# Eighteen more expert tiles' first products made in the gate stage, their outputs kept in device memory until the expert loop

## The chip, the cores and the metric

The kernel runs on one core of one Trainium2 chip. The metric is the device time of one execution in microseconds (us), as the median of a few runs. The core's engines work side by side, each through its own instructions in order: PE (TensorE, the matmuls), PEld (its weight loads, which overlap the matmuls), DVE (VectorE), ACT (ScalarE), POOL (GpSimd) and SP (SyncE, which here only issues DMA transfers). ACT and POOL issue some transfers too. All transfers run on 16 DMA engines.

## The reference, cut to what matters

Two transformer blocks follow one another on 512 tokens of 1024 features. The change touches the last part of the first block, a layer of 16,384 experts of which each token uses 128:

```python
q = einsum('bsd,dq->bsq', h, w_q).reshape(b, s_len, 8, 2, 128)
scores = einsum('bshpc,hpnc->bshpn', q, sub_keys)
# top 16 of each half, top 16 of their 256 sums: 8*16 = 128 experts (best_i) with a softmax weight (gate) each
def token_block(xb, ib, gb):
    u = take(expert_u, ib, axis=0)                     # 16384 x 1024
    act = gelu(einsum('td,tkd->tk', xb, u))
    vv = take(expert_v, ib, axis=0)                    # 16384 x 1024
    return einsum('tk,tkd->td', gb * act, vv)
```

## The kernel before, in words

**Two ways to the same sum.** The first 128 tokens are done by gathering: for each of 128 selections one indirect DMA of 1 MB brings the tokens' rows of `expert_u` and `expert_v` (`gather`, issued by POOL, three buffers), DVE takes a product and sum (`dot`) and later adds the weighted row (`axpy`). The other 384 tokens are done densely: the experts are cut into 128 tiles of 128. For a tile i, `u_chunks` makes the first product, expert_u tile by tokens, in 24 matmuls (three for each of 8 slices, since 32-bit numbers are cut in two parts by `cut`: ACT writes the high part `whi`, DVE or POOL the rest `wlo`), in four chunks of six; `gelu` puts the result, 128 by 384, into `ge`. Then `prepare(i)` multiplies `ge` by the gate weights `gt` of the tile into `pv`, cuts it (`ph`, `pl`), cuts the expert_v tile, and 18 matmuls add tile i's share to `y`, which stays in PSUM through all 128 tiles.

**Stages.** `route` finds the experts of each token (DVE's top 16, POOL's picking). `gates` then writes a dense table of gate weights, 128 experts by 128 tiles by 384 tokens, into device memory (`gscratch`): 12 groups of 8 steps, and in a step DVE builds `oa` and mostly `ob`, PE makes four 32-bit matmuls of 128x128 (`bank`, shown as 8 instructions in the trace), ACT copies the result into `stage`, and after each group ACT issues a 2 MB transfer. The expert loop reads the table back in pieces `gt`, 768 KB for four tiles, in runs of 512 bytes.

**Work ahead.** `ahead` is a generator of the first products of the first tiles; `fill.pull(1)` puts one chunk of it between other PE work. Before, it makes 24 tiles (`STAGES[1]`): 20 in `route`, one at the head of `gates`, and one chunk after every eighth step of `gates`. Then three more tiles are made whole. `AHEAD` is 27: step i of the expert loop makes the first product of tile i+27 and the `y` of tile i, as long as there are such tiles; the last 27 steps have `y` alone. The outputs of 27 tiles wait in SBUF (pools `gep`, 23+1+3 buffers).

**Order.** Within `tc.manual_schedule()` instructions stand in the order of the program; outside it a scheduler places them, and one whole tile made after the gate loop has been moved into it (see the order of PE below). SP issues all loads in one order, and waits there for the buffer of each.

The loop's pace of gathers is `(i + 1) * 5 // 4`: five for four steps. `gate2` makes a piece of the modulation for later, on DVE, from eight rows of `w_ada`.

Of the kernel before, what the change touches and what calls it, by code (L numbers as in the profile page):

```python
# [10 lines left out]
F32 = mybir.dt.float32  # L11
# [4 lines left out]
AF = mybir.ActivationFunctionType  # L16
# [4 lines left out]
P = 128  # L21
# [11 lines left out]
NSEL = PE_H * PE_K  # L33
# [1056 lines left out]
class Block1:  # L1090
# [666 lines left out]
    def peer(self):  # L1757
        c, nc, t, tc = self.c, self.c.nc, self.c.t, self.c.tc
        STAGES = (23, 24, 27)
        AHEAD = STAGES[-1]  # L1760
        GB = 3
        right = ExitStack()
        ND = NB - 1
        TD = ND * P
        with ExitStack() as ctx:
            big = ctx.enter_context(tc.tile_pool(reuse_waits="tile", name="pe", bufs=1))
            up = ctx.enter_context(tc.tile_pool(reuse_waits="tile", name="up", bufs=2))
            gep = [ctx.enter_context(tc.tile_pool(reuse_waits="tile", name="ge", bufs=STAGES[0]))]
# [6 lines left out]
            idx = big.tile([P, NSEL], I32, name="idx")  # L1775
            ge, uraw, ucut = {}, {}, {}

            EARLY, LATE = 14, STAGES[1] - 1
            ahead_u = {"fetch": 0, "cut": 0, "by": nc.gpsimd}

            def spare(u):
# [2 lines left out]
            def fetch_u(last):  # L1784
                for u in range(ahead_u["fetch"], min(last + 1, P)):
                    pool = spare(u)
                    uraw[u] = c.fetch(t["ut"][u], D, pool, 2 if pool is up else 3)
                    ahead_u["fetch"] = u + 1

            def cut_u(last):  # L1790
                for u in range(ahead_u["cut"], min(last + 1, P)):
                    ucut[u] = c.cut(uraw.pop(u), D, spare(u), ahead_u["by"], u == 0)
                    ahead_u["cut"] = u + 1
# [9 lines left out]
                yield lambda: gelu(u, ps)  # L1803

            def gelu(u, ps):
                pool = gep[sum(u % AHEAD >= n for n in STAGES)]
                ge[u] = pool.tile([P, TD], F32, tag="ge", name=c.name("ge"))
                nc.scalar.activation(ge[u], ps[:, :TD], AF.Gelu)

            def ahead():  # L1810
                late = None
                for u in range(STAGES[1]):
                    if u < EARLY:
                        fetch_u(u + 2)
                        cut_u(u + 1)
                    else:
                        fetch_u(min(u + 4, LATE + 1))
                        cut_u(min(u + 3, LATE - (u < LATE - 1)))
                    for x in u_chunks(u):
                        if late is not None:  # L1820
                            late()
                        late = x
                        yield
                late()
                yield
# [25 lines left out]
            def load_g(n):  # L1851
                if n * IC >= P:
                    return
                gt = gts[n] = lp.tile([P, TD // 32, IC, 32], F32, tag="gt", name=c.name("gt"))
                nc.sync.dma_start(gt.rearrange("p g i x -> p g (i x)"),
                                  scratch[:, :, n * IC * 32:(n + 1) * IC * 32].rearrange("g j x -> j g x"))

            def fetch(i):
                if i < P:
                    vraw[i] = c.fetch(t["uv"][i * P:(i + 1) * P, D:], D)  # L1860

            def prepare(i):
                if i >= P:
                    return
                pv = lp.tile([P, TD], F32, tag="pv", name=c.name("pv"))
                ph = lp.tile([P, TD], FR, tag="ph", name=c.name("ph"))
                pl = lp.tile([P, TD], FR, tag="pl", name=c.name("pl"))
                nc.vector.tensor_tensor(out=pv.rearrange("p (g x) -> p g x", x=32),
                                        in0=ge.pop(i).rearrange("p (g x) -> p g x", x=32),
                                        in1=gts[i // IC][:, :, i % IC, :], op=ALU.mult)  # L1870
                vcut[i] = c.cut(vraw.pop(i), D)
                c.split(ph, pl, pv)
                act_in[i] = ph, pl
# [50 lines left out]
                yield  # L1924

            with tc.manual_schedule():
                for u in range(STAGES[1], AHEAD):
                    fetch_u(u + 2)
                    cut_u(u + 1)
                    u_tile(u)()  # L1930
                    if u == STAGES[1]:
                        for i in range(3):
                            fetch(i)
                load_g(0)
                for k in range(GB):
                    gather(k)
                load_g(1)
                prepare(0)
                done = 0
                for i in range(P):  # L1940
                    fetch(i + 3)
                    axpy()
                    prepare(i + 1)
                    fetch_u(i + AHEAD + 2)
                    cut_u(i + AHEAD + 1)
                    if (i + 1) % IC == 0:
                        load_g((i + 1) // IC + 1)
                    while done < min(NSEL, (i + 1) * 5 // 4):
                        dot(done)
                        done += 1  # L1950
                    if i == P - 24:
                        last = gate2()
                    if i >= P - 24 and i % 2:
                        next(last, None)
                    if i + AHEAD < P:
                        u_tile(i + AHEAD)()
                    ph, pl = act_in.pop(i)
                    vh, vl = vcut.pop(i)
                    for b in range(ND):
                        sl = slice(b * P, (b + 1) * P)  # L1960
                        for n in range(2):
                            c.mm3(yd[b][:, n], ph[:, sl], pl[:, sl], vh[:, n * 512:(n + 1) * 512],
                                  vl[:, n * 512:(n + 1) * 512], i == 0, i == P - 1)
                for _ in last:
                    pass
                c.stream.ahead(0)
                axpy()
# [169 lines left out]
    def gates(self, gate, ef, fill):  # L2137
# [6 lines left out]
        with ExitStack() as ctx:  # L2144
# [68 lines left out]
            for n in range(NQ):  # L2213
                g, q = divmod(n, PER)
                if q == PER // 2:
                    digits(g + 1)
                plain(n + 3)
                weighed(n + 2)
                if q == 0:
                    st = gb.tile([P, P, TG], F32, tag="stage", name=c.name("stage"))  # L2220
                ps = self.bank()
                a, b = hot.pop(n), cold.pop(n)
                for e in range(4):
                    nc.tensor.matmul(ps[:, e * P:(e + 1) * P], lhsT=b[:, e], rhs=a[:, e], start=e == 0, stop=True,  # L2224
                                     skip_group_check=True)
                nc.scalar.copy(st[:, :, q * 4:q * 4 + 4], ps.rearrange("p (e x) -> p x e", x=P))
                if q == PER - 1:
                    nc.scalar.dma_start(scratch[g], st.rearrange("p a b -> p (a b)"))
                    fill.pull(1)
        return scratch  # L2230

# [149 lines left out]
```

## Time and profile before

| what | us |
|---|---|
| median of 3 runs | 3203.02 (3199.2 to 3203.53) |
| the profiled execution | 3204.12 |
| its span, first to last instruction | 3202.2 |
| gate loop, first matmul to last | 695.9 to 819.5 |
| expert loop, first `y` matmul to last | 834.9 to 1781.0 |

The span is cut into stages by the trace's clock, which starts with the first instruction. "Busy" of PE is modelled: a matmul's record is longer than the pitch at which the next one starts, so pitches are read from start times. The granted clock (PEclk) of 1.00 is 2.4 GHz and 0.50 is 1.2 GHz.

### The profile page before, as it was taken

What the parts mean: (1) busy time and instruction counts of PE and PEld (TensorE: products, weight loads), DVE (VectorE), ACT (ScalarE), POOL (GpSimd) and SP (SyncE); (2) the same over time, 40 slices, a digit from 0 to 9 for tenths busy, and PEclk for the clock granted to TensorE, in tenths of its full rate; (3) what the DMA queues carried; (4) which work ended last, traced back from release to release, by engine and by line L of the source; (5) the groups of instructions that cost most, each with busy time, mean ns of one, the idle gap of its engine ahead of it and who ended that gap; (6) DMA issues with size and microseconds to landing.
All of it is one profiled execution on the core that took longest, in us unless ns stands there. A gap on an engine that the chain in (4) does not pass through costs nothing.

```text
span 3202.2 us, 44353 instructions
## 1 busy us (share of the span) xinstructions
PE 3001.9 (94%) x17073; PEld 2598.9 (81%) x17073; DVE 2142.7 (67%) x4089; ACT 1293.2 (40%) x2356; POOL 661.9 (21%) x453
## 2 busy tenths in 40 slices
PE   8889987768999999999999999999999989999998
PEld 5666576768899999999988777689999966798896
DVE  6886667789777777777876557655356655555454
ACT  3764342247433333333333334433233266433232
POOL 4432134530112121121110234220000311200001
PEclk9989898979999999999999999999999999999999
DMA  6223321215888888888877211122322201122322
GB/s 214 74 73 99 111 80 66 79 69 220 332 305 303 313 300 318 314 301 310 301 277 235 85 60 39 35 73 91 93 88 83 87 27 32 46 88 87 104 88 84
DMA packets 160805, 479.29 MB, mean 150 GB/s; under 512 B 13489, under 2 KB 68657, under 8 KB 142546
## 3 DMA queue, kind: packets, MB, share of 16 engines
q1 hardware_dynamic: 139346, 316.03, 29.5%
q0 software_dynamic: 18432, 134.23, 11.3%
q10 hardware_dynamic: 2816, 26.22, 2.0%
q8 instruction: 134, 2.20, 0.3%
q14 instruction: 77, 0.63, 0.1%
HBM read 449.15 MB, written 27.27 MB: 149 GB/s over the span
## 4 chain that ended last, share of the span: by engine, by line
PE 73%; DVE 14%; issue 6%; POOL 3%; ACT 3%; DMA 1%; DVEq 0%; SPq 0%; POOLq 0%; ACTq 0%
PE big L171 8%; PE big L173 8%; PE big L172 8%; PE y L172 5%; PE y L173 5%; PE y L171 5%; PE u L171 5%; PE u L173 5%; PE u L172 5%; POOL wlo L152 2%; PE o L596 2%; PE bank L2224 2%; PE bank L172 1%; PE bank L171 1%; PE s L536 1%
## 5 line engine op out<-in xcount | busy, mean ns | idle before, releaser
L152 DVE TENSOR_TENSOR wlo<-wraw,whi 128x1024 fp32r<-128x1024 f32 (+2 forms) x409 | 479.7, 1173 | 530.1 <-ACT whi L151 527.3
L151 ACT CAST whi<-wraw 128x1024 fp32r<-128x1024 f32 (+3 forms) x530 | 524.8, 990 | 704.5 <-PE y L173 267.4
L171 PE MATMUL big<-xh,wlo 128*128 128x264 f32 (+2 forms) x1408 | 421.5, 299 | 4.8 <-POOL wlo L152 4.5
L173 PE MATMUL big<-xh,whi 128*128 128x264 f32 (+2 forms) x1408 | 419.5, 298 | 0.0
L172 PE MATMUL big<-xl,whi 128*128 128x264 f32 (+2 forms) x1408 | 418.7, 297 | 0.0
L152 POOL TENSOR_TENSOR wlo<-wraw,whi 128x1024 fp32r<-128x1024 f32 (+4 forms) x122 | 270.0, 2215 | 717.1 <-ACT whi L151 610.7
L171 PE MATMUL u<-phh,wlo 128*128 128x384 f32 x1024 | 353.4, 345 | 57.6 <-POOL wlo L152 33.4
L172 PE MATMUL u<-phl,whi 128*128 128x384 f32 x1024 | 349.3, 341 | 0.0
L173 PE MATMUL u<-phh,whi 128*128 128x384 f32 x1024 | 349.2, 341 | 0.0
L1878 POOL DMA_INDIRECT g<-in_uv,idx x128 | 160.1, 1251 | 818.7 <-DVE yg L1892 451.1
L173 PE MATMUL y<-whi,ph 128*128 128x512 f32 x768 | 300.8, 392 | 0.0
L172 PE MATMUL y<-wlo,ph 128*128 128x512 f32 x768 | 300.6, 391 | 0.0
L171 PE MATMUL y<-whi,pl 128*128 128x512 f32 x768 | 298.9, 389 | 1.3 <-DVE pl L167 1.3
L171 PEld LDWEIGHTS big<-xh,wlo 128*128 128x128 f32 x1408 | 265.6, 189 | 15.2 <-POOL wlo L152 6.0
L172 PEld LDWEIGHTS big<-xl,whi 128*128 128x128 f32 x1408 | 266.2, 189 | 8.1
L173 PEld LDWEIGHTS big<-xh,whi 128*128 128x128 f32 x1408 | 265.5, 189 | 7.8
L171 PEld LDWEIGHTS u<-phh,wlo 128*128 128x128 f32 x1024 | 197.6, 193 | 67.8 <-POOL wlo L152 38.2
L172 PEld LDWEIGHTS u<-phl,whi 128*128 128x128 f32 x1024 | 197.5, 193 | 4.2
L173 PEld LDWEIGHTS u<-phh,whi 128*128 128x128 f32 x1024 | 196.9, 192 | 0.0
L171 PE MATMUL big<-ah,wlo 128*128 128x264 f32 (+2 forms) x539 | 171.2, 318 | 1.9 <-DVE wlo L152 1.8
L172 PE MATMUL big<-al,whi 128*128 128x264 f32 (+2 forms) x539 | 170.7, 317 | 0.0
L173 PE MATMUL big<-ah,whi 128*128 128x264 f32 (+2 forms) x539 | 170.6, 316 | 0.0
(503 smaller groups left out, 6355.5 us busy)
## 6 DMA issues: line engine op xcount, KB each, us to landing
wraw<-in_ut SPq DMA_DIRECT2D x128, 512.0 KB
wraw<-in_uv SPq DMA_DIRECT2D x128, 512.0 KB
wraw<-in_f_in SPq DMA_DIRECT2D x88, 512.0 KB
gscratch<-stage ACTq DMA_DIRECT2D x12, 2048.0 KB
gt<-gscratch SPq DMA_DIRECT2D x32, 768.0 KB
wada<-in_w_ada SPq DMA_DIRECT2D x40, 512.0 KB
wraw<-in_f_out SPq DMA_DIRECT2D x32, 384.0 KB
wraw<-in_f_out SPq DMA_DIRECT2D x32, 320.0 KB
```

What stands on the lines that cost most here:

```text
L151: self.nc.scalar.copy(hi[:, :n], raw[:, :n])
L152: (engine or self.nc.vector).tensor_tensor(out=lo[:, :n], in0=raw[:, :n], in1=hi[:, :n].bitcast(F32), op=ALU.subtract)
L171: mm(out, lhsT=wl, rhs=xh, start=first, stop=False)
L172: mm(out, lhsT=wh, rhs=xl, start=False, stop=False)
L173: mm(out, lhsT=wh, rhs=xh, start=False, stop=last)
L536: mm(o[:, :n], lhsT=q[:, rows(b)], rhs=k[:, k0:k0 + n], start=True, stop=True)
L596: mm(o[:, j * P:], lhsT=vt[:, j, c0:c0 + w], rhs=at[:, j, j * P:], start=j == 0, stop=False)
L1878: nc.gpsimd.indirect_dma_start(out=g, out_offset=None, in_=t["uv"], in_offset=bass.IndirectOffsetOnAxis(ap=idx[:, k:k + 1], axis=0))
L2224: nc.tensor.matmul(ps[:, e * P:(e + 1) * P], lhsT=b[:, e], rhs=a[:, e], start=e == 0, stop=True, skip_group_check=True)
```

## The change

`ahead` makes 42 tiles in place of 24 (`BEFORE` = 18 + 24). The outputs of the first 18 (`SPILL`) go from ACT to device memory (`spilled`), and come back in the loop (`reload`, issued by SP) into the `pv` buffer that `prepare` then multiplies in place. In `gates` a chunk is pulled after each of the first seven steps of a group, in place of one after the eighth. In the expert loop the first 18 steps and the last 27 have `y` alone (`both` is false), the 83 between have both products; the gathers are paced 17/12 for a step with both and 6/12 for one with `y` alone. `gate2` starts at step 114 in place of 104 and moves on at every step.

```diff
+        SPILL = 18
+        BEFORE = SPILL + STAGES[1]
...
-            EARLY, LATE = 14, STAGES[1] - 1
+            EARLY, LATE = 14, BEFORE - 1
+            spilled = self.dram.tile([SPILL, P, TD], F32, name="gespill")
...
             def gelu(u, ps):
-                pool = gep[sum(u % AHEAD >= n for n in STAGES)]
-                ge[u] = pool.tile([P, TD], F32, tag="ge", name=c.name("ge"))
-                nc.scalar.activation(ge[u], ps[:, :TD], AF.Gelu)
+                r = max(u - SPILL, 0) % AHEAD
+                g = gep[sum(r >= n for n in STAGES)].tile([P, TD], F32, tag="ge", name=c.name("ge"))
+                nc.scalar.activation(g, ps[:, :TD], AF.Gelu)
+                if u < SPILL:
+                    nc.scalar.dma_start(spilled[u], g)
+                else:
+                    ge[u] = g
 
             def ahead():
                 late = None
-                for u in range(STAGES[1]):
+                for u in range(BEFORE):
...
+            def reload(i):
+                if i < SPILL:
+                    ge[i] = lp.tile([P, TD], F32, tag="pv", name=c.name("pv"))
+                    nc.sync.dma_start(ge[i], spilled[i])
+
             def prepare(i):
                 if i >= P:
                     return
-                pv = lp.tile([P, TD], F32, tag="pv", name=c.name("pv"))
+                pv = ge[i] if i < SPILL else lp.tile([P, TD], F32, tag="pv", name=c.name("pv"))
...
-                for u in range(STAGES[1], AHEAD):
+                for u in range(BEFORE, SPILL + AHEAD):
...
                 load_g(1)
+                reload(0)
+                reload(1)
                 prepare(0)
-                done = 0
+                done = due = 0
                 for i in range(P):
                     fetch(i + 3)
                     axpy()
                     prepare(i + 1)
-                    fetch_u(i + AHEAD + 2)
-                    cut_u(i + AHEAD + 1)
+                    reload(i + 2)
+                    both = SPILL <= i < P - AHEAD
+                    if both:
+                        fetch_u(i + AHEAD + 2)
+                        cut_u(i + AHEAD + 1)
                     if (i + 1) % IC == 0:
                         load_g((i + 1) // IC + 1)
-                    while done < min(NSEL, (i + 1) * 5 // 4):
+                    due += 17 if both else 6
+                    while done < min(NSEL, due // 12):
                         dot(done)
                         done += 1
-                    if i == P - 24:
+                    if i == P - 14:
                         last = gate2()
-                    if i >= P - 24 and i % 2:
+                    if i >= P - 14:
                         next(last, None)
-                    if i + AHEAD < P:
+                    if both:
                         u_tile(i + AHEAD)()
...
                 if q == PER - 1:
                     nc.scalar.dma_start(scratch[g], st.rearrange("p a b -> p (a b)"))
+                if q < 7:
                     fill.pull(1)
```

PE in the gate loop, before: the end of one group, its one chunk of a first product (`u`), and the next group.

```order
L2224 MATMUL bank_5116<-oa_5090,ob_5078 128x128 x4
L171 MATMUL u_5123<-phh,wlo_4873 128x384
L172 MATMUL u_5123<-phl,whi_4872 128x384
L173 MATMUL u_5123<-phh,whi_4872 128x384
L171 MATMUL u_5123<-phh,wlo_4873 128x384
L172 MATMUL u_5123<-phl,whi_4872 128x384
L173 MATMUL u_5123<-phh,whi_4872 128x384
L2224 MATMUL bank_5137<-oa_5104,ob_5088 128x128 x4
L2224 MATMUL bank_5147<-oa_5114,ob_5098 128x128 x4
L2224 MATMUL bank_5161<-oa_5134,ob_5112 128x128 x4
```

PE at the same place after the change, in a group's first steps.

```order
L2242 MATMUL bank_5056<-oa_5047,ob_5037 128x128 x4
L171 MATMUL u_5068<-phh,wlo_4891 128x384
L172 MATMUL u_5068<-phl,whi_4890 128x384
L173 MATMUL u_5068<-phh,whi_4890 128x384
L171 MATMUL u_5068<-phh,wlo_4891 128x384
L172 MATMUL u_5068<-phl,whi_4890 128x384
L173 MATMUL u_5068<-phh,whi_4890 128x384
L2242 MATMUL bank_5081<-oa_5049,ob_5039 128x128 x4
L171 MATMUL u_5068<-phh,wlo_4891 128x384
L172 MATMUL u_5068<-phl,whi_4890 128x384
L173 MATMUL u_5068<-phh,whi_4890 128x384
```

Seven steps in eight now have six matmuls of a first product behind them. From the gate loop's first matmul to the first `y` matmul stand 7 tiles of first products before (three of them from the chunks, one that the scheduler moved in, three behind the loop) and 24 after (21 from the chunks, three behind).

SP's transfers where the expert loop begins, before.

```order
L141 DMA wraw_6307<-in_ut 128x1024
L141 DMA wraw_6340<-in_ut 128x1024
L1855 DMA gt_6373<-gscratch 128x12x128
L1855 DMA gt_6381<-gscratch 128x12x128
L141 DMA wraw_6393<-in_uv 128x1024
L141 DMA wraw_6405<-in_ut 128x1024
L141 DMA wraw_6458<-in_uv 128x1024
```

The same place of SP after the change; `pv<-gespill` is a reload.

```order
L141 DMA wraw_6920<-in_ut 128x1024
L141 DMA wraw_6953<-in_ut 128x1024
L1862 DMA gt_6986<-gscratch 128x12x128
L1862 DMA gt_6994<-gscratch 128x12x128
L1872 DMA pv_6996<-gespill 128x384
L1872 DMA pv_6998<-gespill 128x384
L141 DMA wraw_7009<-in_uv 128x1024
L1872 DMA pv_7020<-gespill 128x384
L141 DMA wraw_7040<-in_uv 128x1024
L1872 DMA pv_7051<-gespill 128x384
```

Two reloads stand behind the two pieces of the gate table, and in each of the first steps a reload has the place of an expert_u tile, behind the expert_v tile.

ACT in `route` after the change; before, the same rows stand there without the transfer.

```order
L1811 ACTIVATE ge_3227<-u_3075 128x384
L1813 DMA gespill<-ge_3227 128x384
L2058 COPY sc_3255<-bank_3250 128x512
L2125 COPY pqt_3284<-bank_3259 128x512
L151 CAST whi_3286<-wraw_3156 128x1024
```

All 18 such transfers stand ahead of the gate loop.

## Rows read from the trace of the kernel before

**Rows 1.** The page: span, and busy time of each engine (share of span).

```profile
span 3202.2 us, 44353 instructions
PE 3001.9 (94%) x17073; PEld 2598.9 (81%) x17073; DVE 2142.7 (67%) x4089; ACT 1293.2 (40%) x2356; POOL 661.9 (21%) x453
```

**Rows 2.** By stage: length, busy PE, PEld, DVE, ACT, POOL, PEclk, DMA share, GB/s.

```profile
696.00:819.60 123.60, 109.96 (x860) 105.60 (x858) 116.44 (x199) 95.45 (x216) 0.00 (x0) 0.99 0.53 213
819.60:834.90 15.30, 13.99 (x80) 13.38 (x79) 5.29 (x7) 6.72 (x10) 3.33 (x3) 1.00 0.89 298
834.90:1666.00 831.10, 830.94 (x4200) 756.28 (x4201) 653.86 (x904) 319.55 (x526) 156.75 (x125) 1.00 0.87 310
1690.00:1770.00 80.00, 80.00 (x355) 66.26 (x354) 48.86 (x71) 28.61 (x39) 0.00 (x0) 1.00 0.66 223
```

**Rows 3.** PE in order of time: start, us, instructions, idle before and releaser.

```profile
695.88 5.62 PE L2224 MATMUL bank<-oa,ob 128*128 128x128 f32 x48
...
722.76 2.33 PE L2224 MATMUL bank<-oa,ob 128*128 128x128 f32 x16 [1.20 <-DVE oa L2191]
724.85 0.42 PE L171 MATMUL u<-phh,wlo 128*128 128x384 f32 x1
...
725.98 5.62 PE L2224 MATMUL bank<-oa,ob 128*128 128x128 f32 x48
732.79 2.33 PE L2224 MATMUL bank<-oa,ob 128*128 128x128 f32 x16 [1.20 <-DVE oa L2191]
```

**Rows 4.** PE in order of time, where the scheduler had put a chunk between steps.

```profile
796.64 1.05 PE L2224 MATMUL bank<-oa,ob 128*128 128x128 f32 x8
797.45 0.42 PE L172 MATMUL u<-phl,whi 128*128 128x384 f32 x1
...
798.58 0.38 PE L2224 MATMUL bank<-oa,ob 128*128 128x128 f32 x2
```

**Rows 5.** Groups of the gate loop: busy us, mean ns, idle before.

```profile
L2191 DVE TENSOR_TENSOR oa<-hi,lo 128x512 f32<-128x512 f32 x93 | 61.8, 684 | 0.4 <-PE bank L2224 0.4
...
L152 DVE TENSOR_TENSOR wlo<-wraw,whi 128x1024 fp32r<-128x1024 f32 x3 | 3.7, 1221 | 1.6 <-ACT whi L151 1.6
L151 ACT CAST whi<-wraw 128x1024 fp32r<-128x1024 f32 x3 | 3.1, 1043 | 0.4 <-ACT stage L2226 0.4
L1808 ACT ACTIVATE ge<-u 128x384 f32<-128x384 f32 x3 | 1.5, 489 | 0.9 <-ACT stage L2226 0.9
```

**Rows 6.** Who waited for whom in 500 to 640 (`route`): us, times, longest.

```profile
DVE ef L2091 <- POOL pr L2088: 24.5, 5, 6.1
```

**Rows 7.** The chain that ended last, gate loop's end to the first steps.

```profile
820.43 6.74 DMA gscratch<-stage
...
827.24 4.74 DMA gt<-gscratch
...
834.70 10.64 DMA wraw<-in_ut
```

**Rows 8.** The same stretch in order of time: PE, POOL, DVE, PE.

```profile
819.53 0.42 PE L171 MATMUL u<-phh,wlo 128*128 128x384 f32 x1
...
828.17 1.45 POOL L1878 DMA_INDIRECT g<-in_uv,idx  x1 [141.65 <-ACT whi L151]
...
832.59 0.56 DVE L1868 TENSOR_TENSOR pv<-ge,gt 128x384 f32<-128x384 f32 x1 [4.02 <-DMA gt<-gscratch]
...
834.90 0.47 PE L171 MATMUL y<-whi,pl 128*128 128x512 f32 x1 [0.73 <-DVE pl L167]
```

**Rows 9.** Two stretches of 4 us where the loop begins; columns as rows 2.

```profile
828.00:832.00 4.00, 4.00 (x25) 4.00 (x24) 0.57 (x1) 1.43 (x2) 3.22 (x3) 1.00 0.89 239
836.00:840.00 4.00, 4.00 (x21) 3.43 (x20) 3.69 (x7) 1.95 (x4) 0.00 (x0) 1.00 1.01 416
```

**Rows 10.** DVE's modulation products (`gate2`) in 1690 to 1770.

```profile
L1918 DVE SCALAR_TENSOR_TENSOR junk<-wada,cs 128x1024 bf16<-128x1024 f32 x6 | 7.3, 1219 | 0.0
```

**Rows 11.** PE in `route`, in order of time: the restart after an idle stretch.

```profile
559.66 0.69 PE L171 MATMUL u<-phh,wlo 128*128 128x384 f32 x1 [6.01 <-POOL wlo L152]
...
563.35 0.52 PE L173 MATMUL u<-phh,whi 128*128 128x384 f32 x1
...
563.88 0.33 PE L172 MATMUL u<-phl,whi 128*128 128x384 f32 x1
564.05 0.33 PE L173 MATMUL u<-phh,whi 128*128 128x384 f32 x1
```

More of the change, by code (lines that the diff above doesn't have):

```diff
@@ L1930, in peer @@
                     u_tile(u)()
-                    if u == STAGES[1]:
+                    if u == BEFORE:
                         for i in range(3):
```

## Prediction

> **What bounds the kernel now.** I read the page first: PE is busy 94% of the span [rows 1], so time can only come from the places where PE waits, and a matmul that is moved saves nothing unless it lands in such a wait. Then the stages in a table [rows 2]. In the expert loop PE has no idle time to speak of: 830.94 of 831.10 us while both products are made, 80.00 of 80.00 in the stretch of `y` alone. In the gate loop the fullest engine is DVE, 116.44 of 123.60 us, and PE's 109.96 is modelled. What PE really needs there is read from start times. One group lasts 10.03 us (722.76 to 732.79), with a wait of 1.20 us for DVE's `oa` in it [rows 3]. Six steps run in 5.62 us, which is 0.92 a step when the overhang of the last record is taken off; a step with one chunk behind it lasts 1.94 (796.64 to 798.58) [rows 4]. So eight steps and one chunk are 7 x 0.92 + 1.94 = 8.4 of 10.03 us: PE has only 1.6 us free in a group, some 20 us in the twelve groups, and a chunk costs 1.02. Eighteen tiles are 72 chunks, 73 us. Three quarters of that must lengthen the gate loop.
>
> The last reading is the stretch between the loops, 819.53 to 834.90 [rows 8]. There a chain of transfers rules: the last 2 MB of the table, 6.74 us, then the first piece read back, 4.74 us [rows 7], then DVE's `pv` at 832.59, and `y` 2.31 us later. PE is covered by three first products and idles 0.73 us before `y` [rows 8].
>
> **The gate loop.** After the change a group is seven steps with a chunk and one without: 7 x 1.94 + 0.92 = 14.5 us, twelve groups 174.0. DVE now needs 116.44 / 12 = 9.7 us a group; 18 more `wlo` of 1.22 [rows 5] add 1.8, so it has 11.5 of 14.5. ACT has 95.45 / 12 = 8.0, and 18 more casts and gelus (1.04 + 0.49) add 2.3: 10.3. Both are hidden. What isn't: where a tile's cut stands in the same step as the digits of the next group, ACT's copy and cast, DVE's `wlo`, the digits and `oa` stand in one chain, which is a little longer than the two steps that PE has in hand. I allow one such wait of the 1.2 us seen now for about one tile in seven of the 21: 3.5 us. Bounds are 0 (no wait left) and 7 (a third of the tiles). Gate loop 177.5 us against 123.65 (695.88 to 819.53): **+53.9**, between +50.3 and +57.3.
>
> **The spills.** Eighteen transfers on ACT, all in `route`, each waiting for the gelu just made, which lasts 0.49 [rows 5], and no row shows what it adds: between 0 and that, I say 0.5 us of ACT's time, in front of a copy that DVE's next top 16 needs. I cost them at nothing: DVE waits for POOL there 24.5 us in five waits of up to 6.1 [rows 6], so what comes half a microsecond late waits later half a microsecond less. If that cover were gone they would cost 18 x 0.5 = 9 us.
>
> **Between the loops.** `prepare(0)` now needs the table piece and also `reload(0)`, which SP issues behind both table pieces. Before, `pv` begins at 832.59. The earliest for the reload: the two pieces, 1.57 MB, at the 239 GB/s that moved while they ran alone [rows 9] are 6.6 us from the issue at 827.24, then 0.2 MB in 0.8 us: 834.7, so `y` at 837.0, 17.5 us after the gate loop's end. The latest: it shares the engines with the three gathers that POOL starts at 828.17 [rows 8], 3.1 MB, which at 416 GB/s [rows 9] take 7.6 us: 843.5, `y` at 846, 26.5 us after. The nearest row is the transfer issued at 834.70, which needed 10.64 us with those gathers beside it [rows 7]. I take the middle, 22.3, against 15.37: **+6.9**, between +2.1 and +11.1. PE's three tiles cover 12.5 us, so it idles about 10.
>
> After 6.01 us of idle in `route` PE's matmuls came at a pitch of 0.32 us, not 0.17, for 12 matmuls, the twelfth beginning at 563.35 [rows 11]: the lower granted clock, worth 12 x 0.15 = 1.8 us. The same after the new idle stretch: **+2** (0 if the stretch is short, 3.5 at most, twice that many matmuls).
>
> **The expert loop.** A step with both products lasts 831.1 / 100 = 8.31 us; `y` alone 18 x 80 / 355 = 4.06 [rows 2]. Seventeen tiles fewer behind the first `y`: 17 x 4.25 = **-72.3**. Does PE still bound the steps? DVE: in `y` alone 48.86 less 7.8 us of modulation products (with their read-outs) [rows 10] over 19.7 steps is 2.09; with both 6.54, so a gather costs (6.54 - 2.09 - 1.22) / 1.25 = 2.6. The paces give 2.09 + 0.5 x 2.6 = 3.4 of 4.06 and 3.31 + 1.417 x 2.6 = 7.0 of 8.31: enough. The transfers: with both, a share of 0.87 now [rows 2]; 1/6 of a gather more, 0.17 MB at 416 GB/s, makes it 0.92. The first 18 steps are tight: expert_v 0.52 MB and half a gather 0.52 at 416 GB/s, table piece and reload 0.2 each at 239: 1.26 + 1.26 + 0.82 + 0.82 = 4.17 us for a step of 4.06. In total that is only 18 x 0.11 = 2 us, but each fourth step a table piece of 3.3 us stands on SP's queue ahead of a reload, whose buffer comes free two steps, 8.1 us, before it is wanted. Table piece, expert_v, reload and a gather add up to 7.9. So every fourth step may wait 1 or 2 us. I take **+4**, between 0 (the queue keeps up) and 9.5 (2 us at each of four, and the 2 of the share). `gate2` in the last 14 steps has two products of 1.3 us in three steps of DVE's 2 us: hidden.
>
> **The sum.** +53.9 + 6.9 + 2 - 72.3 + 4 = -5.5 us. The profiled execution took 3204.1, 1.1 more than the median: 3204.1 - 5.5 - 1.1 = **3197.5** for the median. All best ends together give -19.9, all worst +9.1.
>
> **Rivals.**
>
> *The pause and the waits stay away.* The reload is through before the gathers move, the first steps keep up: +52 + 3 - 72.3 + 1 = -16, 3187. For it: in 828 to 832 only 239 GB/s moved though a gather had been issued at 828.17, so the table pieces seem to have gone first [rows 8, 9]. Against: 10.64 us for a transfer a little later [rows 7].
>
> *The engines take turns.* If the DMA engines alternate between SP's and POOL's transfers from the moment both have work, the reload lands with the gathers and each reload in the first steps behind half a gather: +53.9 + 11 + 3 - 72.3 + 7 = +2.6, 3205.6. The Trainium skill states this rule (DMA: Bandwidth & Descriptors, "Queues, rings and completion order": each engine goes round its queues packet by packet). By that rule the time would be 3205.6; the trace agrees with it for the 10.64 us, and rather not for the first 4 us.
>
> *The first eighteen steps are bound by transfers.* This one ends slower: if every reload arrives late, a step lasts what one reload's path lasts divided by its two buffers. At 4.9 us a step the eighteen cost 15 in place of 4, and the time is 3208.5; from 5.0 on it counts as slower. For it: 4.17 against 4.06 before any delay. Against: expert_v has three buffers, and half the steps have no gather.
>
> *The chunks fit into waits that are there anyway.* Then the gate loop would grow by little and some 50 us would be gained, 3150. Only 1.6 of 10.03 us are free [rows 3, 4]; I exclude it.
>
> **Chances.** Forecast, 3192 to 3203 (its own range): 0.50. The pause stays away: 0.22. Turns: 0.18. Transfer-bound first steps: 0.10. A measurement can tell 0.2%, 6.4 us, from no change, which puts the lines at 3196.6 and 3209.4. Below the first lie the second case and nearly half of the forecast's: 0.45. Above the second, most of the last case and a little of the turns: 0.10. The rest 0.45. The range 3187 to 3207 leaves out about 0.2.
>
> **What would show it.** Gate loop: first to last `bank` matmul 177 us, twelve groups at 14.5, few waits of PE for `oa`. Between: `pv` waits for a DMA until about 839 less 819.5, that is 20 us behind the loop's end, PE idle 10 us, PEclk 0.5 behind it. First 18 steps: starts of `y` 4.06 to 4.5 apart, DVE's `pv` waiting for a DMA each fourth time. Then 8.31 a step, without idle. Wrong it would be if PE waits in most gate steps (copies or casts late), if `route` grows by more than 2 us, or if the 1.42 gathers make the steps with both longer than 8.31: each 0.1 there is 8 us.

## The result, and the profile after

| | before | changed |
|---|---|---|
| median (lowest to highest), us | 3203.02 (3199.20 to 3204.12) | 3219.64 (3213.36 to 3221.70) |
| ratio | | 1.0054, 95% interval 1.0043 to 1.0065 |
| span of the profiled execution | 3202.2 | 3216.2 |

The changed kernel is 0.5% slower, 3219.64 where 3197.5 was predicted and 3207 was the upper end. To see where it went, I cut both traces at the same matmuls, by their start times; what a stage gained or lost is the difference of two such differences.

| stage | before | changed | difference | predicted |
|---|---|---|---|---|
| start to the first `u` matmul | 419.9 | 418.6 | -1.3 | 0 |
| route: first `u` to first `bank<-oa` | 276.0 | 285.6 | **+9.6** | 0 |
| gate loop: first to last `bank<-oa` | 123.6 | 177.6 | +54.0 | +53.9 |
| between: last `bank<-oa` to first `y` | 15.4 | 30.4 | **+15.0** | +6.9 |
| expert loop: first to last `y` | 946.1 | 885.2 | **-60.9** | -66.3 (-72.3 + 2 + 4) |
| last `y` to the end | 1421.2 | 1418.7 | -2.4 | 0 |
| span | 3202.2 | 3216.2 | +14.0 | -5.5 |

The two outer stages run the same program in both kernels. They differ from build to build and execution to execution (over the thirteen kernels of this study the first `u` starts at 413.5 to 420.9, and the tail lasts 1414.6 to 1428.0), so stage lengths are compared inside, and medians only over several executions.

First the page of the changed kernel, then its stages [rows 1, 2]: length, busy PE, PEld, DVE, ACT, POOL, PEclk, DMA share, GB/s.

```profile
span 3216.2 us, 44379 instructions
PE 2997.3 (93%) x17073; PEld 2596.7 (81%) x17073; DVE 2173.4 (68%) x4089; ACT 1295.5 (40%) x2356; POOL 670.3 (21%) x453
```

```profile
704.20:881.90 177.70, 175.02 (x1273) 172.99 (x1273) 137.89 (x217) 120.52 (x251) 0.00 (x0) 1.00 0.47 183
881.90:912.20 30.30, 12.68 (x75) 12.39 (x73) 6.91 (x8) 7.11 (x11) 3.04 (x3) 0.78 0.86 313
912.20:993.70 81.50, 75.38 (x306) 60.03 (x306) 57.03 (x84) 26.64 (x42) 7.85 (x8) 0.94 0.81 276
993.70:1683.50 689.80, 689.75 (x3487) 628.00 (x3488) 575.22 (x804) 268.60 (x449) 158.95 (x117) 1.00 0.90 327
```

The gate loop is as forecast: PE is busy 175 of 178 us. The new loss is in the second and third row. PE idles 17.6 us between the loops (30.30 less 12.68), and 6 us in the first 17 steps, where the mean granted clock is 0.94. In the long stretch with both products PE has no idle time, although a step now has 1.42 gathers.

PE in the gate loop [rows 3], one row from each of three groups (start, us, instructions): the last two steps of a group stand together, as the eighth of the one and the first of the next have no chunk between them.

```profile
762.92 1.95 PE L2242 MATMUL bank<-oa,ob 128*128 128x128 f32 x16
...
771.54 1.05 PE L2242 MATMUL bank<-oa,ob 128*128 128x128 f32 x8
...
773.48 1.05 PE L2242 MATMUL bank<-oa,ob 128*128 128x128 f32 x8
...
777.35 1.95 PE L2242 MATMUL bank<-oa,ob 128*128 128x128 f32 x16
```

A step with a chunk is 1.94 us (771.54 to 773.48), a group 14.43 (762.92 to 777.35): the 1.94 and 14.5 of the prediction. PE waits for DVE's `oa` 3.1 us in the whole loop, in eight waits; 3.5 us were allowed for that.

**The route stage.** DVE's waits in the changed kernel, 500 to 650 [rows 6]: total, times, longest.

```profile
DVE wlo L152 <- ACT whi L151: 16.2, 4, 4.1
DVE ef L2109 <- POOL pr L2106: 5.6, 1, 5.6
```

The 24.5 us in which DVE waited for POOL have gone, but nothing became shorter by them. ACT, DVE and POOL in order of time show why; first the kernel before, in one of the steps.

```profile
557.09 0.48 ACT L1808 ACTIVATE ge<-u 128x384 f32<-128x384 f32 x1
557.47 0.58 ACT L2040 COPY sc<-bank 128x512 f32<-128x512 f32 x1
...
559.51 1.23 DVE L152 TENSOR_TENSOR wlo<-wraw,whi 128x1024 fp32r<-128x1024 f32 x1 [3.55 <-ACT whi L151]
...
559.57 6.69 POOL L2086 TENSOR_TENSOR pr<-eq,ci 128x3200 f32<-128x3200 bf16 x1
...
570.03 2.99 DVE L2091 TENSOR_REDUCE ef<-pr 128x64 f32<-128x1600 f32 x1 [4.61 <-POOL pr L2088]
```

The same step in the changed kernel.

```profile
561.83 0.48 ACT L1811 ACTIVATE ge<-u 128x384 f32<-128x384 f32 x1
562.34 0.33 ACTq L1813 DMA_DIRECT2D gespill<-ge  x1
562.71 0.59 ACT L2058 COPY sc<-bank 128x512 f32<-128x512 f32 x1 [0.40 <-ACT ge L1811]
...
564.30 5.64 POOL L2104 TENSOR_TENSOR pr<-eq,ci 128x3200 f32<-128x3200 bf16 x1
...
564.76 6.27 DVE L152 TENSOR_TENSOR wlo<-wraw,whi 128x1024 fp32r<-128x1024 f32 x1 [4.06 <-ACT whi L151]
...
570.03 4.52 POOL L2106 TENSOR_TENSOR pr<-pr 128x1600 f32<-128x1600 f32 x1
```

The spill puts `sc` 0.88 us behind the gelu's start, where it was 0.38. Before, the copy began 0.10 us ahead of the gelu's end; now 0.40 us of idle ACT lie between that end and the copy, and the issue (0.33) stands in them. So DVE's `wlo` of the next w_q tile starts 0.5 us later. Before, it began 0.06 us ahead of POOL's `pr`, and POOL was held for a microsecond (6.69 in place of 5.64). Now it begins 0.46 us behind `pr`, and lasts 6.27 us, until a microsecond after `pr` has ended (564.30 + 5.64 = 569.94, and 571.03). The Trainium skill states the rule (SBUF — State Buffer, "Who interferes with whom"): a VectorE instruction with two SBUF inputs and a GpSimd instruction that reads SBUF contend, and whichever issues second is blocked until the first is through. The rows agree, in both orders.

Alone the half microsecond would have vanished in the wait for POOL, as I had argued, but it brought 5.04 us more of `wlo` with it, and 5.55 is more than the cover of 4.61: `ef` starts at 575.64, 1.1 us after POOL is done. With `ef` no longer waiting, the next small products of DVE also meet POOL's `wlo` (`cv`: seven in 1.58 us, 0.78 before). Two steps last 31.2 us in place of 29.6, five times: 8 of the 9.6 us. Of the other 1.6, 1.2 stand ahead of the first of these five places and 0.4 behind them; their cause stays open.

**Between the loops.** SP's issues in the changed kernel in order of time [rows 7, 8]. ACT issued the last table write at 882.80.

```profile
878.57 1.50 SPq L141 DMA_DIRECT2D wraw<-in_uv  x3
883.57 5.76 SPq L141 DMA_DIRECT2D wraw<-in_ut  x2
894.22 1.08 SPq L1862 DMA_DIRECT2D gt<-gscratch  x2
895.35 3.55 SPq L1872 DMA_DIRECT2D pv<-gespill  x2
```

Two things add up to the 15.0. SP gets past its wait for the write 11.4 us after the write's issue (882.80 to 894.22), where it took 6.8 (820.43 to 827.24); five loads of 0.5 MB, three of expert_v and expert_u tiles 45 and 46, now run beside it. The order of SP's transfers is the same in the kernel before; there four of the five loads were issued 17 us or more ahead of the write, and here all from 4.2 us ahead of it on. That is 4.6. From there to the first `y` it is 18.0 us where it was 7.7: 10.3. The chain that ended last says what in it:

```profile
895.35 14.51 DMA pv<-gespill
```

What the DMA queues moved in that time, q1 for SP and q0 for the gathers (packets, MB, share of the 16 engines' time), from 895 to 901 and then from 901 to 910:

```profile
q1 hardware_dynamic: 2904, 1.48, 92.9%
q0 software_dynamic: 10, 0.08, 4.5%
```

```profile
q0 software_dynamic: 417, 3.05, 82.4%
q1 hardware_dynamic: 487, 0.49, 16.0%
```

POOL issued the gathers from 895.34 on, but they moved next to nothing before 901. Until then SP's queue had the engines almost alone, and brought most of the two table pieces (1.48 of 1.57 MB), which stand ahead of the reload. When the reload's turn came, the gathers had begun: about as many packets of either queue went, but those of the gathers are seven times as large (3.05 MB in 417, 0.49 MB in 487).

**The first steps.** DVE's largest waits from 880 to 1000; the longest is the first `pv`.

```profile
DVE pv L1880 <- DMA pv<-gespill: 27.0, 8, 13.2
```

The first 17 steps take 81.6 us where 17 x 4.08 are 69.4: 12.2 lost. 1.84 of them are the first step at the lower granted clock (5.92 us). The other 10.3 begin with late reloads, seven of the eight waits above; the largest of these, 6.75 us, stopped PE for 4.5 us, and then the granted clock was 0.50 once more. The chain, PE and that step (columns as above):

```profile
947.60 11.71 DMA pv<-gespill
```

```profile
961.54 0.80 PE L171 MATMUL y<-whi,pl 128*128 128x512 f32 x1 [4.51 <-DVE pl L167]
```

```profile
961.54:968.35 6.81, 6.81 (x18) 5.45 (x19) 5.08 (x8) 1.65 (x3) 1.01 (x1) 0.59 0.61 180
```

Twelve of its 18 matmuls came 0.43 us apart or more in place of 0.23, and the step lasted 6.81 us in place of 4.08: 2.7 of the 10.3 us are lost at the lower clock behind that stop, 7.6 in the late reloads themselves. The 17 tiles fewer gave 17 x (8.31 - 4.08) = 71.9, and three short stalls of the kernel before, 1.2 together, are gone: 12.2 - 71.9 - 1.2 = -60.9.

### The profile page after: what moved, and what is told of

Its sections match the earlier page's. It is cut to its first block, busy times and chain, and to the rows that moved or that the text cites. A ratio compares the mean times of both kernels' runs of the same rounds, so it can differ in the third digit from the quotient of the medians.

```text
span 3216.2 us, 44379 instructions
## 1 busy us (share of the span) xinstructions
PE 2997.3 (93%) x17073; PEld 2596.7 (81%) x17073; DVE 2173.4 (68%) x4089; ACT 1295.5 (40%) x2356; POOL 670.3 (21%) x453
## 4 chain that ended last, share of the span: by engine, by line
PE 72%; DVE 14%; issue 5%; POOL 4%; ACT 4%; DMA 1%; SPq 0%; POOLq 0%; DVEq 0%; ACTq 0%
PE big L171 8%; PE big L173 8%; PE big L172 8%; PE y L171 5%; PE y L172 5%; PE y L173 5%; PE u L171 5%; PE u L173 5%; PE u L172 5%; PE bank L2242 2%; POOL wlo L152 2%; PE o L596 2%; PE s L536 1%; DMA pv<-gespill 1%; PE bank L171 1%
## 5 line engine op out<-in xcount | busy, mean ns | idle before, releaser
L152 DVE TENSOR_TENSOR wlo<-wraw,whi 128x1024 fp32r<-128x1024 f32 (+2 forms) x409 | 504.7, 1234 | 524.5 <-ACT whi L151 521.0
L171 PE MATMUL u<-phh,wlo 128*128 128x384 f32 x1024 | 361.2, 353 | 61.3 <-POOL wlo L152 39.1
L1890 POOL DMA_INDIRECT g<-in_uv,idx x128 | 169.8, 1327 | 818.3 <-DVE yg L1904 326.0
L171 PE MATMUL y<-whi,pl 128*128 128x512 f32 x768 | 301.4, 393 | 23.8 <-DVE pl L167 23.7
L171 PEld LDWEIGHTS big<-xh,wlo 128*128 128x128 f32 x1408 | 265.6, 189 | 15.2 <-POOL wlo L152 6.0
L171 PEld LDWEIGHTS y<-whi,pl 128*128 128x128 f32 x768 | 145.4, 189 | 55.2 <-issue 17.9
```

The source lines that it names most:

```text
L152: (engine or self.nc.vector).tensor_tensor(out=lo[:, :n], in0=raw[:, :n], in1=hi[:, :n].bitcast(F32), op=ALU.subtract)
L171: mm(out, lhsT=wl, rhs=xh, start=first, stop=False)
L1890: nc.gpsimd.indirect_dma_start(out=g, out_offset=None, in_=t["uv"], in_offset=bass.IndirectOffsetOnAxis(ap=idx[:, k:k + 1], axis=0))
```

## The experiments

Eleven kernels. "Route", "between" and "17 steps" are the stages above, read from each run's own trace; the gate loop is 177.6 to 177.7 in all that have the change, 123.6 to 123.7 in the two that don't. Each ratio is to executions of the kernel before that were taken together with that run (medians 3202.3 to 3203.8). The stages are those of one execution of each kernel.

| run | median us | ratio to before, 95% interval | route | between | 17 steps |
|---|---|---|---|---|---|
| before | 3203.02 | | 276.0 | 15.4 | |
| changed | 3219.64 | 1.0054 (1.0043 to 1.0065) | 285.6 | 30.4 | 81.6 |
| e1 spills later | 3211.22 | 1.0027 (1.0019 to 1.0036) | 277.0 | 28.4 | 81.9 |
| e2 before, gelu twice | 3211.63 | 1.0028 (1.0016 to 1.0040) | 283.9 | 15.3 | |
| e8 before, short gelu | 3210.60 | 1.0023 (1.0013 to 1.0032) | 284.8 | 15.2 | |
| e3 gathers held | 3223.35 | 1.0071 (1.0058 to 1.0084) | 285.6 | 23.2 | 84.4 |
| e7 the same, 64 bytes | 3227.63 | 1.0078 (1.0061 to 1.0095) | 285.1 | 23.8 | 84.6 |
| e9 the same, no tile | 3213.30 | 1.0032 (1.0022 to 1.0043) | 285.6 | 22.7 | 85.3 |
| e4 pairs | 3201.54 | 1.0002 (0.9993 to 1.0010) | 285.0 | 17.3 | 72.1 |
| e11 pairs, short lead | 3207.22 | 1.0018 (1.0009 to 1.0028) | 285.1 | 19.5 | 85.2 |
| e5 two loads later | 3217.12 | 1.0045 (1.0030 to 1.0061) | 285.7 | 27.9 | 83.2 |
| e6 all three | 3193.46 | 0.9969 (0.9957 to 0.9981) | 276.3 | 20.3 | 72.1 |
| e10 and expert_v sooner | 3189.70 | 0.9957 (0.9943 to 0.9970) | 276.3 | 16.9 | 71.3 |

### The route stage: e1, e2, e8

e1, the spill behind ACT's cast for w_q (`spill` issues what is in `held`):

```diff
                 if u < SPILL:
-                    nc.scalar.dma_start(spilled[u], g)
+                    held.append((u, g))
...
                         wcut[i + 2] = c.cut(wraw.pop(i + 2), D)
+                fill.spill()
```

> The same 18 transfers on ACT, each issued after ACT's cast for the next w_q tile, when ACT has some 12 us to wait, and no longer between the gelu and the copies. Theory A, the half microsecond in ACT's chain puts DVE's wlo behind POOL's pr: the gate loop starts at 696 again (704.2 in the changed kernel), DVE waits for POOL some 24 us in the route stage again, no wlo of 6.3 us; 3219.6 - 8 = 3211.5. Theory B, the transfers themselves slow the loads of the route stage: the start stays at 704, 3219.6.

e2, in the kernel before:

```diff
                 nc.scalar.activation(ge[u], ps[:, :TD], AF.Gelu)
+                if u < 18:
+                    nc.scalar.activation(ge[u], ps[:, :TD], AF.Gelu)
```

> The kernel before, with the gelu of the first 18 tiles done twice on ACT, 0.4 us more at the place where the spill was issued, and no transfer added. Theory A: DVE's wlo falls behind POOL's pr and lasts 6.3 us; two steps of the route stage last 1.2 to 1.6 us longer, five times, so the gate loop starts 6 to 8 us later (702 to 704) and the time is 3209 to 3211. Theory B (the transfers): no change, 3203.

Both came out as theory A says: e1 takes 8.6 us off the route stage with the same 18 transfers, and 3211.2 were measured where 3211.5 were expected; e2 adds 7.9 us without any transfer (3211.6, a little above its range). In e1 DVE waits for POOL again, 500 to 640:

```profile
DVE ef L2115 <- POOL pr L2112: 24.6, 5, 6.1
```

e2 could still mean that each delay adds its own length. So e8 repeats only a sixth of the gelu, `ge[u][:, :64]` from `ps[:, :64]`.

> The kernel before, with a gelu of 64 of the 384 columns once more on ACT at the place of the spill, 0.15 to 0.2 us in place of 0.5, no transfer. Theory A (what costs is the order in which DVE's wlo and POOL's pr start, 0.06 us apart): wlo falls behind pr all the same and lasts 6 us, and the route stage grows by 5 to 8 us as with the whole gelu; 3208 to 3210. Rival L (each delay adds its own length, ten times): 2 us at most, 3205.

The route stage lasts 284.8, 8.8 more than before and a little more than expected; 3210.6 in all. POOL and DVE of e8 in order of time:

```profile
559.15 5.64 POOL L2088 TENSOR_TENSOR pr<-eq,ci 128x3200 f32<-128x3200 bf16 x1
...
559.35 6.53 DVE L152 TENSOR_TENSOR wlo<-wraw,whi 128x1024 fp32r<-128x1024 f32 x1 [3.81 <-ACT whi L151]
```

DVE waits 3.81 us for ACT in place of 3.55: 0.26 us late, half of what the spill made. `wlo` starts 0.20 us behind `pr` and is held all the same. Half the delay costs as much as the whole: it is the order of two starts that were 0.06 us apart, and not ACT's time, that the 8 us are paid for.

### Between the loops: e3, e7, e9

```diff
-                for k in range(GB):
-                    gather(k)
                 load_g(1)
                 reload(0)
                 reload(1)
+                nc.gpsimd.tensor_copy(held, ge[0][:, :1])
+                for k in range(GB):
+                    gather(k)
```

> The changed kernel, where POOL issues the three first gathers only once the first reload has landed (a copy of one column of it on POOL stands ahead of them). Theory T, the reload waits since the engines take turns between the queues: it lands 5 to 8 us after its issue in place of 14.5, and from the gate loop's end to the first y are 22 to 24 us in place of 30.4; the first dot may then wait up to 3 us; 3212 to 3216. Rival S, the reload only stands behind the two table pieces of its own queue: its landing stays 14 us, 3219.6, or later by the late gathers.

The chain of e3 at the same place:

```profile
877.78 10.90 DMA gscratch<-stage
...
889.87 7.39 DMA pv<-gespill
```

The reload lands in 7.39 us in place of 14.51 and `y` begins 7.2 us sooner behind the gate loop: theory T, the gathers. The table pieces stand ahead of the reload in both, and account for most of the 7.39 but not for the 7.1 between the two, so rival S falls. The rows agree with the rule of the Trainium skill that the prediction weighed as a rival (DMA: Bandwidth & Descriptors, "Queues, rings and completion order"): from 901 to 910 in the changed kernel 487 packets of SP's queue went beside 417 of the gathers'.

But the time was 3223, not 3212 to 3216, because of something else: all `y` matmuls were slower, in the last 27 steps too, where there are no gathers. `held` was a new tile of 4 bytes ahead of others in its pool. e7 made it 64 bytes wide, e9 put the copied column into `act`, an existing tile, so that nothing moved.

> The run with the gathers held, with its extra tile 64 bytes wide in place of 4, so that the tiles behind it in that pool start at other addresses. Theory: the 0.23 us (in place of 0.227) of each y matmul there came of the addresses; steps are 8.31 and 4.08 again and the time is 3223.4 - 10 = 3213. Rival: it came of the late gathers; steps stay 8.38 and 4.20, 3223.

> The run with the gathers held, without an extra tile: the copied column goes into the last column of the dots' results, which the last dot overwrites. All tiles of that pool stand at the addresses of the changed kernel. Theory (addresses): y matmuls at 0.227 us again, steps 8.31 and 4.08, gate loop's end to first y 23 us; 3223 - 10 = 3213. Rival (the late gathers): steps stay 8.38 and 4.20, 3223 or more.

My theory on e7 was wrong (a shift of 64 bytes is as bad, 8.38 and 4.20 us a step), and e9, which holds the gathers in the same way but moves nothing, has 8.31 and 4.08 again, and 3213.3 us where 3213 were expected. So the extra tile was the cause and not the late gathers; all that it changes for the `y` matmuls is the addresses of the tiles behind it. PE's `y` matmuls in order of time, of e3 and of e9:

```profile
1699.84 0.40 PE L172 MATMUL y<-wlo,ph 128*128 128x512 f32 x1
1700.08 0.40 PE L173 MATMUL y<-whi,ph 128*128 128x512 f32 x1
1700.31 0.40 PE L171 MATMUL y<-whi,pl 128*128 128x512 f32 x1
```

```profile
1699.67 0.39 PE L172 MATMUL y<-wlo,ph 128*128 128x512 f32 x1
1699.89 0.39 PE L173 MATMUL y<-whi,ph 128*128 128x512 f32 x1
1700.12 0.39 PE L171 MATMUL y<-whi,pl 128*128 128x512 f32 x1
```

In e9 the reload again lands 7.4 us after its issue, and `y` starts 22.7 after the gate loop. Yet of the 7.7 us gained here, the first 17 steps gave back 3.7: the gathers, issued from 901.30 to 905.33, now stood beside the third reload, which needed 12.15 us.

```profile
904.71 12.15 DMA pv<-gespill
```

### The first steps: e4, e11

e4, reloads in pairs, into the two buffers of expert_u tiles that lie idle in the first 18 steps. Two pairs are issued ahead of the table pieces, and in the loop `reload(i + 4)` stands for `reload(i + 2)`; the loads of tiles 45 and 46, which would take those buffers, move to steps 16 and 17.

```diff
-                if i < SPILL:
-                    ge[i] = lp.tile([P, TD], F32, tag="pv", name=c.name("pv"))
-                    nc.sync.dma_start(ge[i], spilled[i])
+                if i < SPILL and i % 2 == 0:
+                    g = up.tile([P, 1024], F32, tag="wraw", name=c.name("back"))
+                    nc.sync.dma_start(g[:, :2 * TD].rearrange("p (m x) -> p m x", m=2),
+                                      spilled[i:i + 2].rearrange("m p x -> p m x"))
+                    ge[i], ge[i + 1] = g[:, :TD], g[:, TD:2 * TD]
...
+                reload(0)
+                reload(2)
                 load_g(0)
```

> The changed kernel with the reloads in pairs into the two buffers of expert_u tiles that are idle in the first 18 steps, issued ahead of the table pieces and three steps ahead of use; the loads of expert_u tiles 45 and 46, which ran beside the last table write, move to steps 16 and 17. Theory T (the reloads come late because of where and when they are issued): 17 us from the gate loop's end to the first y, no wait of pv for a reload, 17 steps at 4.1 (69.7 us in place of 81.6); 3219.6 - 13 - 11 = 3195.5. Rival U, the first steps are bound by the bytes: they stay at 80 us or more, and the time is 3205 or more.

The first `y` stands 17.3 us behind the gate loop (17 expected), no `pv` waits for a reload, and the 17 steps take 72.1: 69.4 and 2.6 for the first step at the lower clock. The bytes are the same, so they were never the bound. The chain of e4, where the table is on it again as in the kernel before [rows 7], and further on what my edit had not foreseen:

```profile
881.25 8.70 DMA gscratch<-stage
890.02 5.14 DMA gt<-gscratch
...
964.49 10.20 DMA wraw<-in_ut
```

Tile 45, now loaded at step 16, came late, and step 17 lasted 13.2 us in place of 8.4. Hence 3201.5, and not 3195.5.

e4 changed lead, size and buffers together. e11 keeps size, buffers and bytes and takes the lead away: `reload(0)` alone ahead of the table, and `reload(i + 2)` in the loop.

> The run with pairs (tiles 45 and 46 at steps 14 and 16), where each pair is issued one step before its use in place of three: same bytes, same buffers, same number of transfers. Theory (what the first steps lacked is lead): pv waits for the reload at each second step, 2 to 4 us each time, and the 17 steps take 85 us or more in place of 72; 3205 or more. Rival (what helped was fewer and larger transfers out of other buffers): they stay near 72 us, some 3197.

85.2 us were measured, 3207.2 in all; e6, with the same pairs, buffers and places of tiles 45 and 46 but the long lead, has 72.1. The waits were not as expected at each second step by 2 to 4 us, but six, 22.0 us together and the longest 9.3. What the first steps lacked was lead.

### Put together: e5, e6, e10

e5 is the changed kernel with tiles 45 and 46 loaded at steps 14 and 16.

> The changed kernel, with the loads of expert_u tiles 45 and 46 moved from beside the last table write to steps 14 and 16; reloads as in the changed kernel. Theory: 1 MB less beside the write lets it land 2.7 us sooner (8.7 as in the run with pairs, 11.4 in the changed kernel), all that follows it comes so much sooner, and the first steps stay at 81.6; 27.7 us from the gate loop's end to the first y; 3217. Rival: the write is limited by itself and lands after 11 us still; 3219.6.

2.5 us less between the loops, 3217.1 where 3217 were expected. But SP still went on only 9.6 us after the write's issue, and e1, with all five loads beside the write, had 9.9 us there and 28.4 between the loops: that e5's edit made the difference is not shown, and the hit may be luck.

> The three edits together: reloads in pairs ahead of the table, tiles 45 and 46 loaded at steps 14 and 16, spills issued after ACT's cast for w_q. Theory: the terms add up; 3201.5 of the run with pairs, less 8.4 in the route stage, less 4.8 at step 17 (13.2 us there, 8.4 expected): 3188, faster than both kernels. Rival: the terms hide one another, or the stages outside take it back as far as the runs scatter; 3195 or more.

Route and steps were as expected, 276.3 and 72.1, and step 17 lasted 8.3. Between the loops it was 20.3 in place of e4's 17.3: SP went on 11.6 us after the write's issue (8.8 in e4), with the three loads of expert_v beside it. 3193.5, better than both kernels, but 5.5 over the 3188, of which these are 3; the 3195 of the rival was not reached either.

In e10 those three loads stand in the gate loop, ahead of tile 39 (`if u == LATE - 2`, in `ahead`).

> The three edits, and the first three expert_v tiles loaded some 25 us sooner, in the gate loop, so that 1.5 MB less run beside the last table write. Theory (the loads beside it delay the write): it lands about 7 us after its issue, as in the kernel before (6.8), in place of 11.6; from the gate loop's end to the first y are 16 us in place of 20.3, and the time is 3193.5 - 4 = 3189.5. Rival (the landing scatters whatever runs beside it): 9 us or more, and no gain.

SP of e10 in order of time; ACT issued the last write at 875.90. Then the stages of e10, columns as above.

```profile
837.05 2.81 SPq L141 DMA_DIRECT2D wraw<-in_uv  x3
861.10 10.51 SPq L141 DMA_DIRECT2D wraw<-in_ut  x2
876.67 5.82 SPq L1883 DMA_DIRECT2D back<-gespill  x2
883.28 1.06 SPq L1877 DMA_DIRECT2D gt<-gscratch  x2
```

```profile
697.20:875.00 177.80, 175.09 (x1273) 173.05 (x1273) 137.91 (x217) 120.43 (x251) 0.00 (x0) 1.00 0.49 190
875.00:891.80 16.80, 12.70 (x75) 12.41 (x73) 5.70 (x7) 6.17 (x10) 3.05 (x3) 1.00 0.92 303
891.80:963.10 71.30, 71.30 (x307) 58.37 (x308) 56.74 (x84) 26.84 (x42) 8.07 (x8) 0.98 0.96 346
963.10:1652.50 689.40, 689.40 (x3488) 627.93 (x3487) 576.09 (x805) 268.89 (x449) 159.22 (x117) 1.00 0.90 329
```

7.4 us from the write's issue to the table's, 4.1 us of idle PE between the loops, none in the first steps: 3189.7, where 3189.5 were expected, 0.43% faster than the kernel before and 0.9% faster than the changed one. Against e6 the two intervals overlap; there the stage, 3.5 us shorter, shows the gain, and not the medians. Over all traces SP went on 6.7 to 6.9 us after the write's issue in the three kernels without the change (before, e2, e8), 7.4 in e10, and 8.8 to 11.7 in the nine with three or five loads beside the write (8.8 in e4 and 11.6 in e6 with the same three: that they cost something is plain, how much within these bounds stays open).

## Why the prediction was wrong

**The gate loop** (+53.9, measured +54.0): right, by its steps; 1.94 us a step, 14.43 a group and 3.1 of waits.

**The spills** (0): the step that failed first. "I cost them at nothing: DVE waits for POOL there 24.5 us in five waits ..." ACT's half microsecond was sized rightly and the wait would have covered it. What the step left out is that a late start changed the order of DVE's `wlo` and POOL's `pr`, and that this order decides which of the two is held. Both rows had to be looked at together; the wait alone, a total of waits above all, doesn't show it. Measured: 9.6 more in the route stage, 8.6 of it given back by e1, and more than the 2 us of `route` that the prediction had named as a sign of being wrong. The price named for a lost cover, 9 us, has the right size by another way, and stood in no chance and no bound of the range.

**Between the loops** (+6.9, bounds 2.1 and 11.1; measured +15.0): two steps failed. I let the last write land as fast as before, though in the changed kernel all five loads ahead of the table are issued at the end of the gate loop and run beside that write: 4.6 us. And "I take the middle", 22.3, between a reload that is first and one that shares the engines. From the table's issue to the first `y` it was 18.0 us, where the middle gives 14.6 and my latest case 18.8. The reload took 14.51 us, in which 351 GB/s moved, and landed with the gathers. That is the second rival's mechanism, to which I gave 0.18 because of one stretch at 239 GB/s [rows 9]; e3 and e9 confirm it. The reading of that stretch was right, the table pieces went first; what I missed is that the reload stands behind them in its own queue and so comes when the gathers begin. Two slips in the working are small beside this: 834.7 and 7.6 make 842.3 and not 843.5, and the middle of 17.5 and 26.5 is 22.0.

**The clock** (+2): right for the idle stretch between the loops, 1.84 us in the first step. The sum had no term for a second stretch at the lower clock, behind a stop of 4.5 us in the first steps: 2.7 us.

**The first 18 steps** (+4, at most 9.5; measured 7.6, and 10.3 with the second stretch at the lower clock): the step that failed is "whose buffer comes free two steps, 8.1 us, before it is wanted". A reload is issued when `pl` of two tiles earlier is done, and wanted as soon as `pl` of the tile in front is: from 929.30 to 934.66 in the trace, 5.4 us, while that reload needed 7.44. For the largest wait it was 6.0 us (946.62 to 952.58) and 11.71. Both stand behind a table piece, as the prediction said; the 7.9 for the transfers and the 8.1 of lead were both too good. The sum of bytes, 4.17 us a step, was no bound: with the same bytes and three steps of lead they take 4.08 (e4), without lead again 85 us (e11). The third rival, transfer-bound steps, had nearly the price (15 us in place of 4). Its picture, a reload's path over two buffers, is near what was found, though only seven reloads were late; its argument from the bytes, 4.17 against 4.06, is not borne out.

**The expert loop** (-72.3): right, -71.9; the faster pace of gathers cost nothing.

With the three failed terms at their measured size (9.6, 8.1 more, 6.3 more) the sum of -5.5 becomes +18.5; the outer stages (-3.7) and the three stalls of the kernel before (-1.2) bring it to the 14.0 between the spans, within 0.4. With their causes removed (e10) the kernel came to 3189.7, near the 3187 of the first rival, which had all of this stay away.

## What to carry to other kernels

Before a delay is costed at nothing because its engine waits later, look at what else starts within the length of that delay, here POOL's `pr` beside DVE's `wlo`: 0.06 us between two starts decided 8 us. What is moved to the end of a stage must not stand beside the transfer for which the next stage waits, and what is needed first is issued early, into buffers that lie idle there: a transfer of 0.2 MB that moved beside three gathers of 1 MB landed with them here. A buffer pair gives a lead of two steps less the time in which a step uses the buffer; that, not the bytes, is to be set against the landing time.

## What the runs showed of the hardware

- Who starts first decides who is held: DVE's `wlo` 1.23 us and POOL's `pr` 6.69 with DVE first by 0.06 us, 6.27 and 5.64 with POOL first by 0.46 us, 6.53 and 5.64 with POOL first by 0.20 us.
- Three gathers issued by POOL from 895.34 on had moved 0.08 MB by 901, and 3.05 MB from 901 to 910.
- A transfer that ACT issues right behind its own gelu puts ACT's next copy 0.50 us later: 0.40 us of idle ACT behind the gelu's end, with the issue's record of 0.33 us in them, and 0.10 us by which the copy had overlapped the gelu. Issued behind the following cast in the program, the same 18 transfers left the route stage at 276.3 (e6, e10) to 277.0 (e1), where it was 276.0 without them.
- `y` matmuls come at 0.233 us in place of 0.227 when a tile of 4 or 64 bytes stands ahead of others in the pool that holds their `ph` and `pl`: 0.07 us in a step with both products, 0.12 in one with `y` alone, 8.3 and 8.5 us in the whole expert loop (897.4 and 897.6 against 889.1; medians 3223.4 and 3227.6 against 3213.3). Which address matters, and why, was not tried.
